# The first four activation tiles moved by 64 bytes within each partition

## The chip, the core and the metric

One core of one Trainium2 chip runs the whole program, once per launch. The metric is the device time of one execution in microseconds (us). Less is better.

## The reference, cut to what matters

The program is a two-layer transformer forward pass on 256 positions of width 2048, in float32. Nearly all of its arithmetic is in products of a 256-row activation with large weight matrices:

```python
def hybrid_mixer(h, w_in, ...):          # layer 1, first part
    p = h @ w_in                         # 2048 x 5136
    ...
    return jnp.concatenate([y_pool, y_dn], axis=-1) @ w_mix_out
def memory_cross_attention(h, mem_h, w_xq, w_xkv, w_xo):
    q = (h @ w_xq).reshape(...)
    kv = mem_h @ w_xkv                   # 2048 x 4096
    ...
    return o @ w_xo
def conv_glu_ffn(h, w_gate, w_up, conv_w, conv_b, w_down):
    gate = causal_dwconv(h @ w_gate, conv_w, conv_b)
    return (jax.nn.silu(gate) * (h @ w_up)) @ w_down
```

The second layer has the same form: an input projection (`w_in_2`), sparse and block attention, an output projection (`w_o_2`) and a feed-forward part of width 8192 (`w_up_2`, `w_down_2`). Around the products stand norms, short convolutions, a gated delta rule, softmaxes, and a modulation by six vectors from `w_ada_2`.

## The kernel before

**The split products.** Each float32 product is done as three passes in the fp32r type. An operand is split into a high part, rounded to fp32r, and a low part, the rest. High times high, high times low and low times high are added up in PSUM; low times low is left out. The split of a weight unit is done in `split_to`: ScalarE writes the high tile `wh` (L220), VectorE writes the low tile `wl` (L222). A unit is 128x1024 values, 512 KB of weights; SyncE's queue loads it into one of four `w32` buffers (L206), up to seven units ahead, and three buffers each of `wh` and `wl` hold split units.

**Two forms of product.** In `lin_b` (lines 320 to 322) a 128x128 block of the weight unit is the stationary operand and the activation, 128x256, is the moving one; the output is transposed. One unit gives 24 matmuls, in triples: `wh` with the high activation (L320), `wh` with the low activation (L321), `wl` with the high activation (L322). In `lin_a` (lines 302 to 304) it is the other way round: a 128x128 block of the activation is stationary and 512 columns of the weights move. Each matmul comes with its own load of the stationary operand into the array (LDWEIGHTS, shown as engine PEld), which runs while the matmul before it still streams.

```python
for b in range(4):
    ps = accs[b // 2][:, (b % 2) * T:(b % 2 + 1) * T]
    wb, wb2 = wh[:, k, b * P:(b + 1) * P], wl[:, k, b * P:(b + 1) * P]
    mm(ps, wb, h, start=kb == 0 and b % 2 == 0, stop=False, skip_group_check=True)
    mm(ps, wb, lo, start=False, stop=False, skip_group_check=True)
    mm(ps, wb2, h, start=False, stop=kb == g.nkb - 1, skip_group_check=True)
```

**The activation tiles.** `act_pair(0)` takes the tiles A0, A1 (high part, 16 blocks of 256 columns) and A2, A3 (low part), 8192 bytes per partition each; `act_pair(1)` takes A4 to A7 in the same way, which `hidden` also uses in pairs. A0 to A3 hold the input of every `lin_b` product but one: the four groups of memory keys (`mk`) read A4 to A7. A0 to A3 are also the stationary operand of some `lin_a` groups (`z0`, `z1`, `w_mix_out`, and the values `nv` and `mv` of layer 2). All other `lin_a` groups (memory values, `w_xo`, `w_down`, `w_o_2`, `w_down_2`) take A4 to A7.

**The order.** All engines' instructions are issued in program order from one Python loop; after each weight unit the loop steps the side tasks once (`pump`): evacuations, norms, attention, the modulation sums. So the tensor engine's queue is a series of units of 24 `lin_b` matmuls or 12 `lin_a` matmuls, with a few matmuls of the side tasks (tiles `m0` to `m3`) between two units.

**Where the tiles lie.** A pool gives each new tag the next free place in the partition, so the order of first use fixes the places, and `pad(name, n)` takes `n` float32 that nobody reads. Before, the byte offset modulo 256 is 128 for A0 to A3 (54656, 62848, 71040 and 79232), 192 for A4 to A7 (87488, 95680, 116416 and 124608), and 192 for all buffers of `wh`, `wl` and `w32` (188352 and up, 4096 bytes each). Between A3 and A4 lie two columns of 32 bytes, `c_mix_p` and `c_mem_p`. Within a tile, every 128-column weight block begins at a multiple of 512 bytes and every 256-column activation block at a multiple of 1024, so a block has its tile's offset modulo 256.

Of the kernel before, what the change touches and what calls it, by code (L numbers as in the profile page):

```python
# [90 lines left out]
class Prog:  # L91
# [409 lines left out]
    def run(self):  # L501
# [65 lines left out]
        self.mhalf = self.pool.tile([P, 8], F32, name="mhalf")  # L567
        nc.gpsimd.memset(self.mhalf, -0.5)
        nc.scalar.activation(self.col("first", 8), self.mhalf, AF.Copy)
        self.pad("pad0", 48)  # L570


        self.split_to(1)
# [9 lines left out]
        def stats():  # L583
            nc.sync.dma_start(cst, i["cst"])
            for c in range(4):
                nc.sync.dma_start(self.X[:, :, c * 512:(c + 1) * 512], xsrc[:, :, c * 512:(c + 1) * 512])
                yield
            self.load_small(w_in, 5120, 16, "ba", "s9")
            for n in ("dn_a_log", "dn_dt_bias"):
                t = self.named[n] = self.col(n, 8)  # L590
                sv = i[n]
                nc.sync.dma_start(t, bass.AP(tensor=sv.tensor, offset=sv.offset, ap=[[0, P], [1, 8]]))
            self.load_const("early")
            for c in range(4):
                for tb in range(2):
                    self.sq_sum(self.X[:, tb, c * 512:(c + 1) * 512], parts[:, tb, c:c + 1])
                yield
            yield from self.rms_task("mix_r", parts, "rr")
            msrc = i["mem"][0].rearrange("(b p) d -> p b d", p=P)
            for c in range(4):  # L600
                mt = self.t("r7", [P, 2, 512])
                nc.gpsimd.dma_start(mt, msrc[:, :, c * 512:(c + 1) * 512])
                for _ in range(3):
                    yield
                for tb in range(2):
                    self.sq_sum(mt[:, tb], mparts[:, tb, c:c + 1])
            self.rcm = self.rms_cols("mem_r", mparts)
            yield
            self.rrm = yield from self.row_bcast(self.rcm, "rrm", 1)

        st = self.start(stats())
        A4 = self.t("A4", [P, 2, 4, T])
        A5 = self.t("A5", [P, 2, 4, T])
        self.pad("pad1", 32)
        S = [{"k": A4[:, 0], "q": A4[:, 1], "v": A5[:, 0]}, {}]
        self.z = [None, None]
# [650 lines left out]
    def ffn1(self, xh, xl, ready, rt):  # L1267
# [6 lines left out]
        def ups(s):  # L1274
            hid[s] = self.hidden(["A4", "A6"] if s % 2 else ["A5", "A7"])
            j = 0
            for c in self.slabs[s]:
                self.lin_b(self.gate[c], xh, xl, lambda a, c=c: self.chain(self.wait_for(rt), self.gate_evac(a, c)),
                           ready=ready if c == 0 else None)
                self.lin_b(self.up[c], xh, xl, lambda a, c=c, j=j: self.up_evac(a, c, j, hid[s]))  # L1280
                j += 4
# [128 lines left out]
    def mixer2(self):  # L1410
# [42 lines left out]
        ev = self.lin_a(b2["nv"], xh, xl, lambda a: self.copy2_evac(a, vsw))  # L1453
        o0h, o0l = self.hidden(["A4", "A6"])
        att = []
# [378 lines left out]
    def ffn2(self):  # L1834
# [8 lines left out]
        def ups(s):  # L1843
            hid[s] = self.hidden(["A4", "A6"] if s % 2 else ["A5", "A7"])
            for c in range(2 * s, 2 * s + 2):
                self.lin_b(self.up2[c], xh, xl, lambda a, c=c: self.relu_evac(a, c, hid[s]),
                           ready=ready if c == 0 else None)
# [91 lines left out]
```

## Time and profile before

| | before |
|---|---|
| median of the runs | 2741.11 us (3 runs, 2740.76 to 2741.56) |
| the profiled execution | 2742.97 us |
| its span, first to last instruction | 2741.2 us |
| mean granted TensorE clock | 0.993 |
| tensor engine (PE) busy | 98% of the span |
| weight loads (PEld), VectorE (DVE), ScalarE (ACT), GpSimd (POOL) busy | 90%, 67%, 47%, 11% |
| read from HBM | 579.21 MB, 212 GB/s over the span |

The profile is of one execution. A matmul's duration is from its start to its modelled end and overlaps the next two matmuls; so durations add up to more than the span, and the pace of the engine is the spacing between starts. In a row of windows each window shows the busy time and, as (x...), the number of instructions that ran in it, those cut by its edges included.

### The profile page before, as it was taken

What the parts mean: (1) busy time and instruction counts of PE and PEld (TensorE: products, weight loads), DVE (VectorE), ACT (ScalarE), POOL (GpSimd) and SP (SyncE); (2) the same over time, 40 slices, a digit from 0 to 9 for tenths busy, and PEclk for the clock granted to TensorE, in tenths of its full rate; (3) what the DMA queues carried; (4) which work ended last, traced back from release to release, by engine and by line L of the source; (5) the groups of instructions that cost most, each with busy time, mean ns of one, the idle gap of its engine ahead of it and who ended that gap; (6) DMA issues with size and microseconds to landing.
All of it is one profiled execution on the core that took longest, in us unless ns stands there. A gap on an engine that the chain in (4) does not pass through costs nothing.

```text
span 2741.2 us, 45609 instructions
## 1 busy us (share of the span) xinstructions
PE 2683.0 (98%) x18322; PEld 2475.7 (90%) x18322; DVE 1848.6 (67%) x2276; ACT 1300.0 (47%) x1894; POOL 289.9 (11%) x249
## 2 busy tenths in 40 slices
PE   8999999999999999999999989999989999999997
PEld 8999998889989999999999789998879988999896
DVE  6665745677787877777877576677576566655556
ACT  6544533454455455444444454444554444444443
POOL 0230201000001020000000031101121000000020
PEclk9999999999999999999999999999999999999999
DMA  8644544688787877877877745443557767665554
GB/s 289 200 127 133 187 124 139 221 293 273 230 269 263 273 259 256 282 261 271 277 264 257 216 148 178 152 141 125 178 174 239 238 217 241 232 190 190 192 185 145
DMA packets 292116, 584.29 MB, mean 213 GB/s; under 512 B 23968, under 2 KB 32288, under 8 KB 291904
## 3 DMA queue, kind: packets, MB, share of 16 engines
q1 hardware_dynamic: 287952, 569.93, 63.5%
q0 software_dynamic: 3232, 10.14, 1.2%
q8 instruction: 143, 2.34, 0.3%
q10 hardware_dynamic: 720, 1.31, 0.1%
q14 instruction: 69, 0.57, 0.1%
HBM read 579.21 MB, written 2.10 MB: 212 GB/s over the span
## 4 chain that ended last, share of the span: by engine, by line
PE 89%; issue 6%; DVE 2%; ACT 1%; POOL 1%; DMA 0%; SPq 0%; DVEq 0%; ACTq 0%; POOLq 0%
PE acc L320 16%; PE acc L321 16%; PE acc L322 16%; PE acc L302 11%; PE acc L303 11%; PE acc L304 11%; PE m L992 1%; DVE wl L222 1%; PE m L1045 1%; PE m L1052 1%; ACT wh L220 1%; PE m L1142 1%; PE m L1111 1%; PE m L995 0%; DMA w<-w_in 0%
## 5 line engine op out<-in xcount | busy, mean ns | idle before, releaser
L222 DVE TENSOR_TENSOR wl<-w,wh 128x1024 fp32r<-128x1024 f32 x874 | 1094.3, 1254 | 826.4 <-ACT wh L220 820.0
L220 ACT ACTIVATE wh<-w 128x1024 fp32r<-128x1024 f32 x880 | 928.6, 1059 | 1152.7 <-PE acc L321 618.6
L320 PE MATMUL acc<-A,wh 128*128 128x256 f32 x3968 | 1125.1, 284 | 11.4 <-ACT A L406 7.7
L322 PE MATMUL acc<-A,wl 128*128 128x256 f32 x3968 | 1113.4, 281 | 6.1 <-POOL wl L222 3.3
L321 PE MATMUL acc<-A,wh 128*128 128x256 f32 x3968 | 1113.6, 281 | 0.4 <-DVE A L407 0.2
L320 PEld LDWEIGHTS acc<-A,wh 128*128 128x128 f32 x3968 | 752.0, 190 | 13.4 <-ACT A L406 7.7
L322 PEld LDWEIGHTS acc<-A,wl 128*128 128x128 f32 x3968 | 757.4, 191 | 6.7 <-POOL wl L222 3.7
L321 PEld LDWEIGHTS acc<-A,wh 128*128 128x128 f32 x3968 | 750.5, 189 | 2.2 <-DVE A L1406 0.6
L302 PE MATMUL acc<-wh,A 128*128 128x512 f32 x1536 | 608.6, 396 | 3.5 <-ACT wh L220 3.2
L303 PE MATMUL acc<-wl,A 128*128 128x512 f32 x1536 | 600.9, 391 | 2.2 <-DVE wl L222 2.2
L304 PE MATMUL acc<-wh,A 128*128 128x512 f32 x1536 | 600.6, 391 | 0.0
L303 PEld LDWEIGHTS acc<-wl,A 128*128 128x128 f32 x1536 | 289.4, 188 | 63.0 <-DVE wl L222 5.2
L302 PEld LDWEIGHTS acc<-wh,A 128*128 128x128 f32 x1536 | 289.1, 188 | 62.6 <-ACT wh L220 3.6
L304 PEld LDWEIGHTS acc<-wh,A 128*128 128x128 f32 x1536 | 289.1, 188 | 61.1
L1194 DVE SCALAR_TENSOR_TENSOR r<-r,c_silu_c,r 128x1024 f32<-128x1024 f32 x128 | 170.0, 1328 | 0.0
L1828 POOL TENSOR_TENSOR s<-s 128x512 f32<-128x512 f32 x32 | 51.0, 1593 | 557.2 <-ACT s L1827 557.2
L1194 DVE SCALAR_TENSOR_TENSOR s<-s,c_silu_c,s 128x512 f32<-128x512 f32 x128 | 95.8, 749 | 13.4 <-DMA s<-w_ada 11.6
L1249 POOL TENSOR_TENSOR r<-r,rr 128x1024 f32<-128x1024 f32 x11 | 27.9, 2534 | 571.8 <-ACT r L1248 529.0
L1672 ACT ACTIVATE s<-s,c_am 128x128 f32<-128x128 f32 (+1 forms) x48 | 21.5, 448 | 92.2 <-DVE c_am L1670 92.2
L1560 POOL TENSOR_TENSOR r<-r,s 128x512 f32<-128x512 f32 x15 | 25.5, 1703 | 227.4 <-DVE s L1557 227.4
L1245 DVE SCALAR_TENSOR_TENSOR r<-r,prm,r 128x254 f32<-128x254 f32 x88 | 42.3, 481 | 1.6
L378 ACT ACTIVATE dd<-X 128x512 bf16<-128x512 f32 x40 | 25.1, 627 | 23.2 <-DVE X L441 15.8
(368 smaller groups left out, 1634.7 us busy)
## 6 DMA issues: line engine op xcount, KB each, us to landing
w<-w_up SPq DMA_DIRECT2D x216, 512.0 KB, 3.7
w<-w_down SPq DMA_DIRECT2D x216, 512.0 KB, 4.0
w<-w_in SPq DMA_DIRECT2D x152, 512.0 KB, 3.5
r<-w_ada SPq DMA_DIRECT2D x128, 512.0 KB, 5.0
w<-w_gate SPq DMA_DIRECT2D x88, 512.0 KB, 4.3
w<-w_xkv SPq DMA_DIRECT2D x64, 512.0 KB, 3.9
s<-w_ada SPq DMA_DIRECT2D x128, 256.0 KB, 5.0
w<-w_mix_out SPq DMA_DIRECT2D x32, 512.0 KB, 3.6
```

The lines of the kernel that those rows point to most:

```text
L220: nc.scalar.activation(hi[:, :m], src[:, :m], AF.Copy)
L222: eng.tensor_tensor(lo[:, :m], src[:, :m], hi[:, :m].bitcast(F32), op=OP.subtract)
L302: mm(ps, h, wh[:, k, :], start=kb == 0, stop=False)
L303: mm(ps, h, wl[:, k, :], start=False, stop=False)
L304: mm(ps, lo, wh[:, k, :], start=False, stop=kb == g.nkb - 1)
L320: mm(ps, wb, h, start=kb == 0 and b % 2 == 0, stop=False, skip_group_check=True)
L321: mm(ps, wb, lo, start=False, stop=False, skip_group_check=True)
L322: mm(ps, wb2, h, start=False, stop=kb == g.nkb - 1, skip_group_check=True)
L1194: nc.vector.scalar_tensor_tensor(acc, tiles.pop(n), self.silu_c[:, kb:kb + 1], acc, op0=OP.mult, op1=OP.add)
L1245: nc.vector.scalar_tensor_tensor(cv[:, b, s:], st[:, b, :T - s], w[k], cv[:, b, s:], op0=OP.mult, op1=OP.add)
L1249: nc.gpsimd.tensor_tensor(cv, cv, self.rr[:, None, :].to_broadcast([P, 4, T]), op=OP.mult)
L1828: nc.gpsimd.tensor_tensor(y, y, y, op=OP.mult)
```

## The change

The pad ahead of A0 shrinks from 48 to 32 float32, and a new pad of 16 float32 stands between `c_mem_p` and A4:

```diff
-        self.pad("pad0", 48)
+        self.pad("pad0", 32)
...
         st = self.start(stats())
+        self.pad("pad3", 16)
         A4 = self.t("A4", [P, 2, 4, T])
```

A0 to A3 and the two 32-byte columns behind them begin 64 bytes earlier: A0 to A3 at 64 modulo 256. A4 and all tiles after it stay where they were. No instruction is added, removed or put in another order; the addresses in those that read or write A0 to A3, `c_mix_p` and `c_mem_p` are all that differs. Modulo 256, the distance from the weight buffers (192) to A0 to A3 goes from 64 to 128.

## Rows read from the trace of the kernel before

**Rows 1.** The profile's first part (busy time by engine) and its chain that ended last.
```profile
PE 2683.0 (98%) x18322; PEld 2475.7 (90%) x18322; DVE 1848.6 (67%) x2276; ACT 1300.0 (47%) x1894; POOL 289.9 (11%) x249
...
PE 89%; issue 6%; DVE 2%; ACT 1%; POOL 1%; DMA 0%; SPq 0%; DVEq 0%; ACTq 0%; POOLq 0%
```

**Rows 2.** Instruction groups of PE: shape, count, busy us, mean ns of one.
```profile
L320 PE MATMUL acc<-A,wh 128*128 128x256 f32 x3968 | 1125.1, 284 | 11.4 <-ACT A L406 7.7 <-ACT A L1401 3.5 <-ACT wh L220 0.2
L321 PE MATMUL acc<-A,wh 128*128 128x256 f32 x3968 | 1113.6, 281 | 0.4 <-DVE A L407 0.2
...
L302 PE MATMUL acc<-wh,A 128*128 128x512 f32 x1536 | 608.6, 396 | 3.5 <-ACT wh L220 3.2 <-DVE r L1258 0.3
```

**Rows 3.** Timeline of PE, three lin_b stretches; each pair is 8 spacings apart.
```profile
1299.74 0.28 PE L321 MATMUL acc<-A,wh 128*128 128x256 f32 x1
...
1300.65 0.28 PE L320 MATMUL acc<-A,wh 128*128 128x256 f32 x1
...
897.83 0.28 PE L321 MATMUL acc<-A,wh 128*128 128x256 f32 x1
...
898.77 0.28 PE L320 MATMUL acc<-A,wh 128*128 128x256 f32 x1
...
330.77 0.28 PE L321 MATMUL acc<-A,wh 128*128 128x256 f32 x1
...
331.73 0.28 PE L320 MATMUL acc<-A,wh 128*128 128x256 f32 x1
```

**Rows 4.** All engines in three windows of lin_b: us, then PE, PEld, DVE, ACT, POOL.
```profile
1300.00:1342.00 42.00, 42.00 (x373) 42.00 (x372) 33.61 (x37) 19.81 (x23) 0.79 (x1) 1.00 0.79 265
898.00:950.00 52.00, 52.00 (x443) 52.00 (x443) 42.70 (x46) 23.88 (x27) 2.44 (x1) 1.00 0.81 270
330.00:336.00 6.00, 6.00 (x52) 6.00 (x52) 2.56 (x3) 2.12 (x2) 0.00 (x0) 1.00 0.57 170
```

**Rows 5.** Line 321 alone, by stretch: PE busy (matmuls), PEld busy, clock, DMA.
```profile
13.00:236.00 223.00, 140.84 (x505) 94.96 (x505) 1.00 0.60 187
294.00:420.00 126.00, 72.45 (x256) 49.10 (x256) 1.00 0.48 146
613.00:1077.00 464.00, 251.22 (x894) 168.01 (x895) 1.00 0.79 263
1122.00:1212.00 90.00, 71.10 (x254) 47.72 (x255) 1.00 0.78 265
1256.00:1477.00 221.00, 141.74 (x511) 95.95 (x511) 1.00 0.81 273
1591.00:1863.00 272.00, 139.82 (x500) 94.90 (x500) 0.99 0.53 160
2016.00:2104.00 88.00, 69.22 (x251) 47.08 (x251) 1.00 0.72 238
2148.00:2637.00 489.00, 214.98 (x767) 144.01 (x767) 1.00 0.65 211
```

**Rows 6.** PEld groups in the windows 1300:1342, 898:950 (two rows) and 330:350.
```profile
L320 PEld LDWEIGHTS acc<-A,wh 128*128 128x128 f32 x124 | 23.3, 188 | 0.0
...
L320 PEld LDWEIGHTS acc<-A,wh 128*128 128x128 f32 x148 | 28.4, 192 | 0.0
L322 PEld LDWEIGHTS acc<-A,wl 128*128 128x128 f32 x148 | 27.8, 188 | 0.0
...
L322 PEld LDWEIGHTS acc<-A,wl 128*128 128x128 f32 x41 | 7.9, 192 | 0.0
```

**Rows 7.** Timeline of lin_a: first pair 9 spacings apart, second pair 10.
```profile
274.74 0.40 PE L303 MATMUL acc<-wl,A 128*128 128x512 f32 x1
...
276.81 0.39 PE L303 MATMUL acc<-wl,A 128*128 128x512 f32 x1
...
1229.67 0.39 PE L302 MATMUL acc<-wh,A 128*128 128x512 f32 x1
...
1231.94 0.39 PE L303 MATMUL acc<-wl,A 128*128 128x512 f32 x1
```

**Rows 8.** Writes of the activation tiles A, duration in ns min/median/max.
```profile
L406 ACT ACTIVATE A<-r,prm x32: 489/494/511, 7.1 to 300.9; 128x256 fp32r<-128x256 f32 x32
```

## Prediction

> **What bounds the kernel now.** I read the page first. The tensor engine is busy for 98% of the span, and the chain that ended last is PE for 89% [rows 1]. So the time is very nearly the number of matmuls times their spacing; a change of address can pay or cost only through the spacing, unless it slows a writer.
>
> Then the groups. The three lines of `lin_b` have 3968 matmuls each, of mean 281 to 284 ns, the three of `lin_a` 1536 each [rows 2]. A mean hides levels, so I looked at starts one after the other. Within one shape, with no wait between matmuls and the clock fully granted, there are three spacings [rows 3]: 0.91 us for eight starts (114 ns) around 1300 us, 0.94 us (117.5 ns) around 898 us, and 0.96 us (120 ns) around 331 us. The longer windows sharpen them. A window counts also what is in flight at its left edge, some 2.5 matmuls, so 42.00 us hold about 370.5 (113.4 ns), and 52.00 us about 440.5 (118.0 ns) [rows 4]. For the third I keep the 120 ns of the starts, since 6.00 us for 49.5 is too short to be better. With the levels go durations of 276, 281 and 283 ns, by which I can tell them in any row: 294 to 420 us has 72.45 us for 256, which is 283.
>
> The first two levels are A0 to A3 against the weights, 64 bytes apart modulo 256. The third, 120 ns, holds through all of 294 to 420 us: the only `lin_b` groups that read A4 to A7, at the same offset as the weights, distance 0. Loads of the stationary operand tell the same story: 188 ns each at 113.4 ns spacing; one line of the three at 192 ns at 118; at 120 ns the load of L322 has 192 ns as well [rows 6]. So I read the levels as two read streams of the tensor engine, the moving activation and the next weight block, getting into each other's way: always at distance 0; at distance 64 sometimes, in a manner that lasts for whole stretches.
>
> **How much time the 118 ns level takes.** Line 321 alone by stretch [rows 5]. Against 276 ns each, the seven stretches of A0 to A3 (all but 294 to 420) have: 140.84 - 505 x 0.276 = 1.5 us; 251.22 - 246.7 = 4.5; 71.10 - 70.1 = 1.0; 141.74 - 141.0 = 0.7; 139.82 - 138.0 = 1.8; 69.22 - 69.3 = -0.1; 214.98 - 211.7 = 3.3. Together 12.7 us on 3682 matmuls. One at the 118 ns level is 5 ns longer, so 12.7 / (3682 x 0.005) = 69% are at it. Three lines have 11046 matmuls; 69% of them by 4.6 ns of spacing (118.0 - 113.4) is 35 us. A few of those durations are long for other reasons (the stretch from 1591 has clock 0.99), so I take 33 us as what `lin_b` on A0 to A3 loses now against the 113.4 ns level.
>
> **The change part by part.**
>
> *The moving operand of lin_b.* The change removes and adds no instruction; it puts the moving operand of 11046 matmuls 128 bytes modulo 256 from the weights. No row shows this distance. Bounds from the nearest rows: all at 113.4 gives -33 us; all at 120, as at distance 0, gives 0.31 x 11046 x 6.6 ns = +22.6 and 0.69 x 11046 x 2.0 ns = +15.2, together +38 us. I take the lower end: from distance 0 to 64 the rows go from 120 ns throughout to 113.4 ns in part, 128 is the farthest that two offsets can be apart modulo 256, and a disturbance that fades with distance should be gone there.
>
> *What is behind it.* If PE goes faster, split units must come faster: 24 matmuls at 118.0 ns are 2.83 us, at 113.4 ns 2.72 us. In the window at 898 us DVE is busy 42.70 of 52.00 us (82%), ACT 46%, the DMA engines 81% [rows 4]. At 113.4 ns these become some 85%, 48% and 84%; the window at 1300 us already runs so, at 79% DMA and no idle PE. This cover stays. In stretches with many side matmuls (13 to 236 and 1591 to 1863 us) PE waits now and then for others, and part of the gain will be eaten there. Those hold 3.3 of the 12.7 us; with half of that lost, 13%, -33 becomes -29 us.
>
> *The stationary operand of lin_a.* The `lin_a` groups on A0 to A3 are 288 of the 1536 per line, 864 matmuls. At 275 us they are spaced 2.07 us / 9 = 230 ns, while groups on A4 to A7 at 1230 us have 2.27 / 10 = 227 ns [rows 7]. Here distance 0 is the better one, so the new distance may bring -3 ns or another +3 ns: -2.6 to +2.6 us. I take 0, for the two signs have equal support.
>
> *The writers.* ACT fills A0 to A1 and, later, A4 to A5 with the same instruction, 16 times each; over all 32 the duration is 489 to 511 ns [rows 8], so an offset of 128 or 192 makes no more than 22 ns. Most of these writes run beside matmuls; on the path stand a few at the start of each layer part, below 0.2 us. I take 0. The two 32-byte columns take sums of ACT and are read once each: 0.
>
> *The sum.* Span 2741.2 - 29 = 2712 us. The profiled execution took 2742.97, 1.8 more than its span, and the median is 1.9 below that; so the same 2712 for the median.
>
> The Trainium skill speaks against the whole change ("TensorE: Matmul & The Clock Gate", section "Step-by-step: what each phase is for"): the engine has two independent SBUF read ports, and loading the next weights does not take read bandwidth from the running matmul. By that page there would be nothing to gain from offsets, and the sum would be 0. The trace does not agree as far as spacing goes: one shape has 113.4, 118.0 and 120 ns in [rows 3, 4].
>
> **The rivals.**
>
> *No change: the offset is not the cause.* Which level a stretch has may be set by how the stretch begins (the first matmuls after side work) and the tiles' places may have nothing to do with it. For: at one and the same distance, 64, both levels occur, and they switch. Against: the 120 ns level belongs to A4 to A7 through 126 us and many interruptions, while no stretch of A0 to A3 has a mean above 281 [rows 5]. The time would be 2741, give or take 5 us for another draw of the levels. The rule of the Trainium skill named above ("TensorE: Matmul & The Clock Gate", same section) would give the same time; by the three spacings the trace speaks against it.
>
> *Slower: what counts repeats every 128 bytes.* Then 128 apart is as bad as 0 apart, all of `lin_b` runs at 120 ns, and the price is the +38 us above, less 2.6 us in `lin_a`: 2776 us. Place: L320 to L322 on A0 to A3. It decides as soon as the mean spacing there is over today's mean of 0.69 x 118.0 + 0.31 x 113.4 = 116.6 ns, a mean duration of 279.4 ns. For: distance 0 and 64 differ, and nothing in the rows shows that 64 and 128 aren't the two halves of one period. Against: two levels at distance 64 look like a middle case, not like the far end.
>
> *Slower by less: the 118 ns level becomes the lasting one.* If the new distance has both levels but falls into the 118 ns one nearly always, the 31% that have 113.4 ns now cost 4.6 ns each: 11046 x 0.31 x 4.6 = +16 us, 2757 us. For: stretches at 118 ns today tend to stay there (613 to 1077 us has a mean of 251.22 / 894 = 281 ns [rows 5]). Against: 2016 to 2104 us stays at 276 ns just as well.
>
> **How the numbers follow.** Forecast, 113.4 ns nearly everywhere: 0.48. No change: 0.17. 118 ns nearly everywhere: 0.18. The 128-byte repeat: 0.17. The predicted time is 2712, with 2706 to 2730 as its own range (all 33 us and the 2.6 of `lin_a` saved, or a third of the gain). A measurement of this kernel can tell some 0.2%, 5.5 us, from no change. Of the no-change case a little falls to either side, so faster is 0.49, same 0.15, slower 0.36. For 8 in 10 the range takes the forecast, the no-change case and the 118 ns case, and leaves the 120 ns case out: 2706 to 2762.
>
> **What would show it.** In the profile after: L320, L321 and L322 at a mean of 276 to 277 ns outside 294 to 420 us, all their loads at 188 ns, and windows like 898 to 950 us with 2.72 us for a unit of 24. From 294 to 420 us must stay at 283 ns, for neither A4 to A7 nor the weights move. DVE and ACT durations must not move. The forecast is wrong if the mean of L321 over A0 to A3 stays at 279 ns or rises; 283 ns with 192 ns loads would say that the repeat is 128 bytes, and 281 ns that the 118 ns level has won. The 113.4 ns level with an unchanged time would say that I misjudged the cover: then idle PE ahead of L320 with `wl` or `wh` as releaser must have grown.

## The result, and the profile after

| | before | after |
|---|---|---|
| median, timed in turn on one chip | 2741.16 us (4 runs, 2740.76 to 2741.56) | 2772.02 us (4 runs, 2771.12 to 2773.87) |
| span of the profiled execution | 2741.2 us | 2769.3 us |
| mean granted TensorE clock | 0.993 | 0.993 |

The ratio is 1.0111, with a 95% interval of 1.0099 to 1.0123: slower by 31 us. That is 60 us above the forecast, 10 us outside its range, and 4 us under the rival of a 128-byte repeat.

The page of after, the lines that answer to [rows 1] (busy time and count by engine; shares of the chain that ended last):

```profile
PE 2716.5 (98%) x18322; PEld 2507.4 (91%) x18322; DVE 1848.6 (67%) x2276; ACT 1300.6 (47%) x1894; POOL 288.8 (10%) x249
...
PE 89%; issue 6%; DVE 2%; ACT 1%; POOL 1%; DMA 0%; DVEq 0%; SPq 0%; ACTq 0%; POOLq 0%
```

PE is busy 33.5 us longer with the same 18322 matmuls. VectorE and ScalarE have the same busy time, and the clock is the same. PE's idle time went from 2741.2 - 2683.0 = 58.2 to 52.8 us, so 28 of the 33.5 us reach the span of these two executions. Nothing waits longer; the matmuls come more slowly. Which ones, the groups of after say (busy us, mean ns; as [rows 2]):

```profile
L320 PE MATMUL acc<-A,wh 128*128 128x256 f32 x3968 | 1131.6, 285 | 11.2 <-ACT A L406 7.7 <-ACT A L1402 3.5
L322 PE MATMUL acc<-A,wl 128*128 128x256 f32 x3968 | 1125.8, 284 | 5.8 <-POOL wl L222 3.1 <-DVE wl L222 2.7
L321 PE MATMUL acc<-A,wh 128*128 128x256 f32 x3968 | 1124.3, 283 | 0.1
L302 PE MATMUL acc<-wh,A 128*128 128x512 f32 x1536 | 609.2, 397 | 3.7 <-ACT wh L220 3.4 <-DVE r L1259 0.3
```

`lin_b` has it: L321 takes 10.7 us more than before, at a mean of 283 ns in place of 281 (the memory keys included in both). By stretch, L321 alone in four of the eight stretches (PE busy and matmuls, PEld busy and loads, clock, DMA share, GB/s; as [rows 5]):

```profile
296.00:422.00 126.00, 72.14 (x256) 48.85 (x255) 1.00 0.49 145
616.00:1085.00 469.00, 253.29 (x896) 168.82 (x896) 1.00 0.80 260
...
1265.00:1493.00 228.00, 143.93 (x511) 96.17 (x511) 1.00 0.81 265
...
2031.00:2126.00 95.00, 72.53 (x255) 48.79 (x256) 0.98 0.68 222
```

The first is the memory keys, which read A4 to A7: still 282 to 283 ns. The three others read A0 to A3 and have 253.29 / 896 = 283, 282 and 284 ns, where before they had 281, 277 and 276. The 284 is in part the clock: the granted clock was 0.5 (1.2 GHz) for 3.4 us at the start of that row, whose mean is 0.98; from 2036 us on, at 1.00, it is 69.43 us for 247, 281 ns. So the stretches that were at the best level lost most, some 5 ns against 2. The timeline of PE in after, each pair ten spacings apart, first on A0 to A3 (1.19 us, 119 ns), then in the memory keys (1.20 us, 120 ns):

```profile
909.83 0.28 PE L322 MATMUL acc<-A,wl 128*128 128x256 f32 x1
...
911.02 0.28 PE L320 MATMUL acc<-A,wh 128*128 128x256 f32 x1
...
330.76 0.28 PE L321 MATMUL acc<-A,wh 128*128 128x256 f32 x1
...
331.96 0.28 PE L322 MATMUL acc<-A,wl 128*128 128x256 f32 x1
```

Over all starts on A0 to A3 that follow each other within 140 ns (some 11,000), worked out from the trace, the mean spacing is 116.2 ns before and 119.2 after. 3.0 ns x 11046 = 33 us, about all that PE's busy time grew by. After is not the mix of 113.4 and 118, and not the steady 120 of the memory keys either: most single spacings lie between 115 and 122 ns.

Taken by group (the 192 matmuls that add up one set of outputs), after has two lasting levels as before has: 118.7 and 120.0 ns in place of 113.3 and 117.8. All engines in 20 us of two groups, first in before, then in the same two groups of after (columns as in [rows 4]):

```profile
1034.00:1054.00 20.00, 20.00 (x172) 20.00 (x172) 14.61 (x15) 8.58 (x9) 0.00 (x0) 1.00 0.80 277
2062.00:2082.00 20.00, 20.00 (x179) 20.00 (x179) 11.65 (x11) 9.61 (x12) 3.20 (x2) 1.00 0.77 247
...
1040.00:1060.00 20.00, 20.00 (x169) 20.00 (x168) 14.23 (x15) 8.58 (x9) 0.00 (x0) 1.00 0.82 268
2082.00:2102.00 20.00, 20.00 (x171) 20.00 (x170) 10.96 (x11) 9.31 (x11) 3.19 (x2) 1.00 0.75 239
```

Of the 58 groups on A0 to A3, all 13 that before has within 0.25 ns of 113.4 are at 118.7 in after, and of the 27 at 117.8, 21 are at 120.0. So the offset sets what the two levels are; which of the two a group gets goes largely with its place in the program.

Two more lines of after: the loads of one line in the window from 905 to 955 us, and the writers (as [rows 8]):

```profile
L320 PEld LDWEIGHTS acc<-A,wh 128*128 128x128 f32 x141 | 26.5, 188 | 0.0
...
L406 ACT ACTIVATE A<-r,prm x32: 489/494/512, 7.2 to 302.4; 128x256 fp32r<-128x256 f32 x32
```

At 119 ns the loads still take 188 ns, so a load's duration doesn't tell the level. The writers have not moved. In `lin_a` on A0 to A3, spacing went from 229.4 to 232.5 ns: 3.1 x 864 = 2.7 us. Starts of side matmuls that follow each other sum to 213.8 us in this execution of before and 209.4 in after, which takes more than that off again.

### The profile page after: what moved, and what is told of

It is laid out like the page before. It is cut to its first block, busy times and chain, and to the rows that moved or that the text cites. A ratio compares the mean times of both kernels' runs of the same rounds, so it can differ in the third digit from the quotient of the medians.

```text
span 2769.3 us, 45609 instructions
## 1 busy us (share of the span) xinstructions
PE 2716.5 (98%) x18322; PEld 2507.4 (91%) x18322; DVE 1848.6 (67%) x2276; ACT 1300.6 (47%) x1894; POOL 288.8 (10%) x249
## 4 chain that ended last, share of the span: by engine, by line
PE 89%; issue 6%; DVE 2%; ACT 1%; POOL 1%; DMA 0%; DVEq 0%; SPq 0%; ACTq 0%; POOLq 0%
PE acc L322 16%; PE acc L321 16%; PE acc L320 16%; PE acc L302 11%; PE acc L303 11%; PE acc L304 11%; PE m L993 1%; DVE wl L222 1%; PE m L1046 1%; PE m L1053 1%; PE m L1112 0%; PE m L1143 0%; ACT wh L220 0%; PE m L996 0%; PE m L1701 0%
## 5 line engine op out<-in xcount | busy, mean ns | idle before, releaser
L320 PE MATMUL acc<-A,wh 128*128 128x256 f32 x3968 | 1131.6, 285 | 11.2 <-ACT A L406 7.7
L322 PE MATMUL acc<-A,wl 128*128 128x256 f32 x3968 | 1125.8, 284 | 5.8 <-POOL wl L222 3.1
L321 PE MATMUL acc<-A,wh 128*128 128x256 f32 x3968 | 1124.3, 283 | 0.1
L320 PEld LDWEIGHTS acc<-A,wh 128*128 128x128 f32 x3968 | 754.0, 190 | 13.1 <-ACT A L406 7.7
L322 PEld LDWEIGHTS acc<-A,wl 128*128 128x128 f32 x3968 | 752.3, 190 | 6.4 <-POOL wl L222 3.5
L321 PEld LDWEIGHTS acc<-A,wh 128*128 128x128 f32 x3968 | 751.3, 189 | 1.9 <-DVE A L1407 0.6
```

## The experiments

"Distance" below is the weight tile's offset minus the activation tile's, modulo 256: 64 before, 128 after, 0 in the memory keys. "Spacing" is the mean on A0 to A3, worked out as above, from one start to the next. Edits are made to the kernel before, if nothing else is said. Each kernel was timed beside the kernel before, which had a median of 2738.0 to 2742.6 us; brackets after a ratio are its 95% interval.

### Is it the distance, and does it repeat after 128 bytes?

Two kernels put A0 to A3 at the other two multiples of 64; a third leaves A0 to A3 at after's place and moves everything behind them, the weights included, by the same 64 bytes.

```diff
# e1_at0 (e2_at192: no pad0, pad3 of 48)
-        self.pad("pad0", 48)
+        self.pad("pad0", 16)
...
         st = self.start(stats())
+        self.pad("pad3", 32)
# e3_all64
-        self.pad("pad0", 48)
+        self.pad("pad0", 32)
```

> A0 to A3 at 0 modulo 256, 64 bytes from the weights (192) on the other side than before; A4 and all later tiles unmoved. Theory D256 (the spacing follows the distance from moving to stationary operand modulo 256): a level of its own for this fourth distance; if it is the mirror of the kernel before, 2741 us, otherwise anything from 2710 to 2780. Theory D128 (the distance counts modulo 128): the same as before, 2741 within 6 us. Theory OWN (the offset of the moving tile itself counts, whatever the weights do): no tie to 2741.

> A0 to A3 at 192 modulo 256, at the same offset as the weights, distance 0 as in the memory-key groups. D256 and D128: lin_b on A0 to A3 goes to the 120 ns spacing of those groups (durations 283 ns, loads 192 ns), lin_a on them to 227 ns: about 2741 + 38 - 3 = 2776 us. D128 adds that this is the level of the changed kernel. OWN would allow another level.

> A0 to A3 at 64 as in the changed kernel, but without the second pad, so that A4 to A7, the weights and all tiles behind A3 move down by 64 bytes too: weights and A4 to A7 at 128, distance from A0 to A3 again 64 as before. Any theory of distance: as before, 2741 within 6 us. OWN: as the changed kernel, 2772 within 6 us.

Measured: at 0, 2755.6 us, 1.0055 [1.0035, 1.0076], spacing 117.7; at 192, 2776.8 us, 1.0130 [1.0111, 1.0150], spacing 119.9; all moved, 2739.2 us, 0.9996 [0.9985, 1.0006], spacing 116.2. The timeline of PE in the kernel with distance 0 (offset 192), 18 spacings in 2.16 us, and then the loads of L321 from 905 to 955 us:

```profile
904.79 0.28 PE L322 MATMUL acc<-A,wl 128*128 128x256 f32 x1
...
906.95 0.28 PE L322 MATMUL acc<-A,wl 128*128 128x256 f32 x1
...
L321 PEld LDWEIGHTS acc<-A,wh 128*128 128x128 f32 x140 | 26.9, 192 | 0.0
```

120.0 ns with 192 ns loads throughout: distance 0 gives A0 to A3 what it gives the memory keys, at the 2776 us that the prediction had worked out for 120 ns everywhere. With everything moved, after's place for A0 to A3 costs nothing. So the relative offset counts, not the tiles' own place. And the repeat is not 128 bytes: distance 192 (offset 0) ought then to be like 64, and it is 14 us slower, with nearly uniform spacings of 117 to 119 in place of the mix.

### What lies between?

Four kernels at the 32-byte steps, by the same two pads (`e6_at96` 40 and 8, `e7_at32` 24 and 24, `e8_at224` 8 and 40; `e9_at160` 40 and 8, with the two 32-byte columns moved ahead of `pad0`).

```diff
# e7_at32
-        self.pad("pad0", 48)
+        self.pad("pad0", 24)
...
+        self.pad("pad3", 24)
# e9_at160
-        self.pad("pad0", 48)
+        parts, mparts = self.parts("mix_p"), self.parts("mem_p")
+        self.pad("pad0", 40)
...
-        parts, mparts = self.parts("mix_p"), self.parts("mem_p")
...
+        self.pad("pad3", 8)
```

> A0 to A3 at 96 modulo 256, half way between the kernel before (128) and the changed one (64); everything else unmoved. Theory LINE (what counts is in which 64-byte piece a block begins): the same as at 64, 2772 us within 6. Theory FINE (the distance counts in steps below 64 bytes): between the two, 2745 to 2768 us, with a spacing of its own.

> A0 to A3 at 32 modulo 256, half way between 0 (2756 us, 117.7 ns) and 64 (2772 us, 119.2 ns). LINE: as at 0, 2756 us. FINE: between, 2756 to 2772 us.

> A0 to A3 at 160 modulo 256 (the two small columns go ahead of the pad), half way between 128 (2741 us, 116.2 ns) and 192 (2777 us, 119.9 ns). LINE: as at 128, 2741 us. FINE: between, 2741 to 2777 us; a spacing of 113.4 ns throughout would give 2712 us and a better place than any so far.

> A0 to A3 at 224 modulo 256, the last of the eight steps of 32 bytes, half way between 192 (2777 us) and 0 (2756 us). FINE, with what the other three half steps showed: a level of its own, 2755 to 2785 us. If the best distance were plus or minus 32 from the weights (160 is minus 32 and had 2762 us): under 2741 us.

All eight places together (weights at 192):

| A0 to A3 at | distance | us | ratio | spacing, ns |
|---|---|---|---|---|
| 128 (before) | 64 | 2741.2 | 1 | 116.2 |
| 224 | 224 | 2748.4 | 1.0027 [1.0017, 1.0037] | 116.8 |
| 0 | 192 | 2755.6 | 1.0055 [1.0035, 1.0076] | 117.7 |
| 160 | 32 | 2762.4 | 1.0077 [1.0060, 1.0094] | 118.3 |
| 96 | 96 | 2763.2 | 1.0079 [1.0064, 1.0094] | 118.3 |
| 64 (after) | 128 | 2772.0 | 1.0111 [1.0099, 1.0123] | 119.2 |
| 192 | 0 | 2776.8 | 1.0130 [1.0111, 1.0150] | 119.9 |
| 32 | 160 | 2780.3 | 1.0143 [1.0128, 1.0158] | 120.0 |

Steps of 32 bytes count, which the 64-byte theory denied; but the finer theory, by which a place lies between its neighbours, failed as well. Distance 160 is worse than both 128 and 192, distance 224 better than both 192 and 0. I found no formula over the distance, and which level belongs to which distance stays a table. The time does follow the spacing: 3.8 ns between the best and the worst row, by 11046, are 42 us, and the medians differ by 39.

### High and low tiles at different distances

The high tiles A0 and A1 (L320, L322) and the low ones A2 and A3 (L321) are set 64 bytes apart.

```diff
# e4_hi64: A0, A1 at 64; A2, A3 at 128 (e5_lo64: A2, A3 first, then pad3, then A0, A1)
-        a = [self.t(f"A{4 * half + j}", [P, 8, T], F32R) for j in range(4)]
+        a = [self.t(f"A{4 * half + j}", [P, 8, T], F32R) for j in range(2)]
+        if not half and "apart" not in self.named:
+            self.named["apart"] = self.pad("pad3", 16)
+        a += [self.t(f"A{4 * half + j}", [P, 8, T], F32R) for j in (2, 3)]
...
-        self.pad("pad0", 48)
+        self.pad("pad0", 32)
```

> Half of the change: A0 and A1 (high part, moving in two of three lin_b matmuls) at 64, A2 and A3 (low part, moving in one of three) stay at 128. If each matmul loses by its own moving tile, two thirds of the loss of 31 us: about 2762 us. If the load of the wl block, which runs beside the low part, were the one that collides, there would be no loss: 2741 us.

> The other half of the change: A2 and A3 (low part) at 64, A0 and A1 (high part) at 128, the weights at 192. With the high part alone at 64 the time was 2777 us, more than with both (2772). Theory EACH (each matmul loses by its own moving tile): one third of 31 us, 2751 us. Theory STEP (unequal offsets of high and low part are bad in themselves, since the moving stream then jumps in its place modulo 256 at every second matmul): 2770 to 2785 us.

Measured: 2776.9 us, 1.0129 [1.0105, 1.0153], and 2766.4 us, 1.0090 [1.0074, 1.0107]. Both miss all that was expected. Low at 128 and high at 64 is worse than all four at 64; its spacings, from a matmul's own start to the next, are 119.4, 121.2 and 119.2 ns for L320, L321 and L322, so the low tiles, which had not moved, have the longest. The three lines don't each bring the price of their own distance: both mixtures cost more than their share. This spoke for something that carries over from one matmul to the next.

### Is it the load beside the stream?

The other stream in the engine is the load of the next weight block. Three kernels shorten it: the stationary block has 32 columns in place of 128, and the matmul writes 32 output rows, so that three quarters of those products are left out. The moving operand and the number of matmuls stay. `e10_short` shortens two lines of three; the next two shorten all three lines of `lin_b` in all blocks but the first of a group.

```diff
# e10_short, on the kernel after
-                    mm(ps, wb, lo, start=False, stop=False, skip_group_check=True)
-                    mm(ps, wb2, h, start=False, stop=kb == g.nkb - 1, skip_group_check=True)
+                    mm(ps[:32], wb[:, :32], lo, start=False, stop=False, skip_group_check=True)
+                    mm(ps[:32], wb2[:, :32], h, start=False, stop=kb == g.nkb - 1, skip_group_check=True)
# e11_short_after and e12_short_before, ahead of the three mm
+                    n = 32 if kb else P
+                    ps, wb, wb2 = ps[:n], wb[:, :n], wb2[:, :n]
```

> The changed kernel, with the second and third matmul of each lin_b triple (L321, L322) using only the first 32 of 128 stationary columns, so that their loads are a quarter as long; the moving streams stay. It leaves out three quarters of these two passes. Theory LOAD (the moving stream loses while a load of the stationary operand runs): two of three collisions shrink to a quarter, the spacing of lin_b on A0 to A3 falls from 119.2 to 113.4 + 5.8 x (1 + 0.25 + 0.25) / 3 = 116.3 ns or less, the time to about 2740 us or less. Theory MOVING (the moving streams alone set the level): 119 ns and 2772 us as the changed kernel.

> The changed kernel, with all three matmuls of a lin_b triple using only 32 of 128 stationary columns in 15 of the 16 blocks of a product (three quarters of lin_b's outputs are left out there); moving streams and order stay. LOAD: the spacing on A0 to A3 is at most 113.4 + 5.8 / 4 = 114.9 ns, the time 2772 less 11046 x 4.3 ns = about 2724 us, and no more than 8 us above the same edit on the kernel before. MOVING: the difference of the two kernels of 31 us stays, at 2772 us here.

> The same shortening of all lin_b loads on the kernel before (A0 to A3 at 128). LOAD: spacing 113.4 + 2.8 / 4 = 114.1 ns, time about 2741 - 11046 x 2.1 ns = 2718 us, no more than 8 us under the changed kernel with this edit. MOVING: 2741 us, 31 us under it.

Measured: 2744.0 us, 1.0010 [1.0000, 1.0021], spacing 116.7; 2730.9 us, 0.9962 [0.9947, 0.9977], spacing 115.6; 2714.9 us, 0.9902 [0.9887, 0.9917], spacing 113.9. First two load groups of `e10_short`, from 905 to 955 us, then the timeline of `e12_short_before`, 19 spacings in 2.16 us:

```profile
L320 PEld LDWEIGHTS acc<-A,wh 128*128 128x128 f32 x143 | 26.9, 188 | 1.3
L322 PEld LDWEIGHTS acc<-A,wl 128*32 128x32 f32 x144 | 15.5, 108 | 1.1
```

```profile
904.74 0.28 PE L323 MATMUL acc<-A,wh 128*32 128x256 f32 x1
...
906.90 0.28 PE L324 MATMUL acc<-A,wl 128*32 128x256 f32 x1
```

Loads of 108 in place of 188 ns bring 113.7 ns by these two rows, the 113.4 ns level within their rounding; no group in any kernel here has a mean below 113.3. The load, or the writing of 128 output rows in place of 32, is thus a part of it, since the moving stream did not change; the next section tells the two apart. Between after and before there remained 16 us with short loads, where the theory of the load allowed 8 and that of the moving stream alone wanted 31. The 8 was worked out with loads a quarter as long, though, and they were 108 / 188 = 57% as long: a loss in proportion to the load's duration would have left 18 of the 31 us. So these three runs refute the theory of the moving stream alone, but not that of the load.

### Moving the loads instead of the stream

If the pair of stream and load counts, then the same must come from moving the load alone. First the short loads were displaced, by 192 bytes in after and by 64 in before (64 bytes either way, modulo 256), to other columns of the same weight block (so other products are computed; three quarters are left out as above):

```diff
# e13_after_c48, on the kernel after (e14_before_c16, on before: c = 16)
+                    n, c = (32, 48) if kb else (P, 0)
+                    ps, wb, wb2 = ps[:n], wb[:, c:c + n], wb2[:, c:c + n]
```

> The changed kernel with short loads as in e11_short_after, but of columns 48 to 79 of each block in place of 0 to 31, so that the load begins 192 bytes further on; A0 to A3, all tiles and the moving streams stay at the changed places. The distance from moving to loaded operand is then as in the kernel before (64 below). Theory PAIR (the level is set by the distance of the two streams that run side by side): the level of e12_short_before, 2715 us within 5, 113.9 ns. Theory PLACE (the offset of the moving stream itself, with the rest): as e11_short_after, 2731 us within 5, 115.4 ns.

> The kernel before with short loads of columns 16 to 47, which begin 64 bytes further on; all tiles where they were before, distance of moving to loaded operand 128 as in the changed kernel. PAIR: the level of e11_short_after, 2731 us within 5, 115.4 ns. PLACE: as e12_short_before, 2715 us within 5, 113.9 ns.

Measured: 2730.2 us, 0.9954 [0.9937, 0.9971], and 2712.7 us, 0.9895 [0.9880, 0.9910]. The times did not move, against the theory of the pair. The spacings did in after. All engines in 20 us of two groups that follow each other, first in `e11_short_after`, then in `e13_after_c48`:

```profile
980.00:1000.00 20.00, 20.00 (x176) 18.57 (x174) 15.97 (x12) 7.92 (x8) 3.23 (x2) 1.00 0.81 269
1002.00:1022.00 20.00, 20.00 (x176) 18.56 (x174) 18.70 (x21) 10.42 (x12) 2.43 (x1) 1.00 0.86 277
...
984.00:1004.00 20.00, 20.00 (x174) 18.42 (x172) 15.80 (x12) 7.91 (x8) 3.08 (x2) 1.00 0.81 270
1006.00:1026.00 20.00, 20.00 (x179) 19.03 (x178) 19.00 (x21) 10.46 (x12) 2.42 (x1) 1.00 0.85 277
```

With the short loads at their own places most groups run at 115.8 ns. Displaced, most go in turn at 116.8 and 113.7, whose mean is 115.3. That the two kernels take the same time is thus two different patterns with nearly one mean; no run shows a reason for it.

Then all loads at full length, each reading 128 columns that begin 16 columns (64 bytes) beside its block, so that neighbouring weight columns are multiplied; the work is all there, and no tile moves.

```diff
# e15_after_off192, on the kernel after: loads at 128 modulo 256
-                    wb, wb2 = wh[:, k, b * P:(b + 1) * P], wl[:, k, b * P:(b + 1) * P]
+                    o = k * g.n + b * P
+                    o += 48 if o == 0 else -16
+                    wb, wb2 = (w.rearrange("p k c -> p (k c)")[:, o:o + P] for w in (wh, wl))
# e16_before_off64, on the kernel before: loads at 0 modulo 256
+                    o += -48 if o == 896 else 16
```

> The changed kernel with full loads again (128 columns), each displaced in the weight tile by 192 bytes modulo 256 (16 columns earlier, for the first block of a unit 48 later), so each lin_b matmul uses neighbouring weight columns in place of its own. All tiles and moving streams stay at the changed places; the distance from moving to loaded operand is that of the kernel before. In the short-load runs one block in 16 still had full loads at the old places, which may have set the level for the 15 others. PAIR: 2741 us within 6, 113 to 118 ns mixed. PLACE: 2772 us within 6, 119 ns. In the memory keys the distance becomes that of e1_at0, which may take 2 us off in both.

> The kernel before with full loads displaced by 64 bytes modulo 256 (16 columns later, for the last block of a unit 48 earlier), so each lin_b matmul uses neighbouring weight columns. All tiles stay where they were before; the distance from moving to loaded operand is that of the changed kernel. PAIR: 2772 us within 6, 119 ns. PLACE: 2741 us within 6, 116 ns. In the memory keys up to 3 us less in both.

Measured: 2736.5 us, 0.9994 [0.9985, 1.0003], spacing 115.9; 2763.6 us, 1.0095 [1.0078, 1.0112], spacing 118.8. All engines from 905 to 955 us (PE, PEld, DVE, ACT, POOL, clock, DMA share, GB/s) in the kernel before, in the kernel after, in `e15_after_off192` and in `e16_before_off64`:

```profile
905.00:955.00 50.00, 50.00 (x427) 50.00 (x426) 41.06 (x44) 23.71 (x27) 2.44 (x1) 1.00 0.82 275
```

```profile
905.00:955.00 50.00, 50.00 (x424) 50.00 (x423) 41.29 (x44) 22.66 (x26) 2.39 (x1) 1.00 0.83 275
```

```profile
905.00:955.00 50.00, 50.00 (x443) 50.00 (x443) 42.87 (x46) 25.29 (x28) 2.81 (x2) 1.00 0.85 288
```

```profile
905.00:955.00 50.00, 50.00 (x424) 50.00 (x423) 40.59 (x44) 24.02 (x27) 2.40 (x1) 1.00 0.82 271
```

After with displaced loads starts 19 more matmuls in 50 us, PE never idle in either: (443 - 2.5) in 50 us are 113.5 ns, (424 - 2.5) are 118.6. This window is one in which `e15_after_off192` has the better level and before the worse (427); over all starts on A0 to A3, 119.2 ns became 115.9. By group the levels change places as well: after with displaced loads has 113.3 and 117.8 ns, the two of before, and before with displaced loads has 118.7 in most groups, the lower one of after. The load's address alone gives after's time back, and takes most of it from before: 22 of 31 us by the medians, 26 if each is set against the kernel before on its own chip (2763.6 - 2738.0), a little less than was expected. Some 3 us of the rest are hidden by the memory keys, which the same edit makes faster (119.8 to 115.8 ns, 768 matmuls). So the pair was right, for loads at full length.

The two kernels hold a test that I had not planned. Displaced loads also change the distance in the memory keys, whose activation tiles the change never touches: from 0 to 192 in the first, to 64 in the second. The timelines, 23 spacings each, 2.71 us (117.8 ns) in the first and 2.61 us (113.5 ns) in the second:

```profile
330.17 0.28 PE L324 MATMUL acc<-A,wl 128*128 128x256 f32 x1
...
332.88 0.28 PE L323 MATMUL acc<-A,wh 128*128 128x256 f32 x1
```

```profile
330.29 0.28 PE L324 MATMUL acc<-A,wl 128*128 128x256 f32 x1
...
332.90 0.28 PE L323 MATMUL acc<-A,wh 128*128 128x256 f32 x1
```

At distance 0 it was 120 ns. 117.8 is what distance 192 gave on A0 to A3 (117.7), and 113.5 is the better level of distance 64; over all memory keys the means are 117.8 and 115.8 ns, against 117.7 and 116.2 in the table. So two rows of the table hold for other tiles in another place. They also bear on the period: modulo 512, the distances of this 192 and of the one in `e1_at0` differ by 256 bytes, and the spacing is the same.

### Why did displaced short loads leave the time as it was?

In the kernels with short loads, the first block of each group still has full ones: 3968 - 3720 = 248 of 3968 per line, 6%. These were not displaced above. Now they alone are, by 64 bytes, and the short ones stay (three quarters of the short products are left out, and in the full ones neighbouring columns are multiplied).

```diff
# e17_after_set, on the kernel after (e18_before_set, on before: + (16 if kb == 0 else 0))
+                    n = 32 if kb else P
+                    o = k * g.n + b * P + ((-16 if b else 48) if kb == 0 else 0)
+                    ps, wb, wb2 = ps[:n], *(w.rearrange("p k c -> p (k c)")[:, o:o + n] for w in (wh, wl))
```

> The changed kernel with short loads as in e11_short_after (columns 0 to 31 at their own places, distance 128 to the moving operand), and only the full loads of the first of 16 blocks displaced by 192 bytes modulo 256 to the old distance. Theory SET (the full loads set the level, and the stream keeps it through the 15 blocks with short loads): the time of e12_short_before, 2715 us within 5. Theory RUN (each short load acts where it is): as e11_short_after, 2731 us within 5.

> The same on the kernel before: short loads at their own places (distance 64), the full loads of the first block displaced by 64 bytes to the distance of the changed kernel. SET: the time of e11_short_after, 2731 us within 5. RUN: as e12_short_before, 2715 us within 5.

Measured: 2714.7 us, 0.9899 [0.9885, 0.9914], spacing 114.0; 2728.3 us, 0.9945 [0.9929, 0.9962], spacing 115.3. The two kernels have changed places: after with displaced full loads stands where before with short loads stood (2714.9), and the reverse (2730.9). Instruction groups of the line `wh` with the low activation, first in `e17_after_set`, then in `e18_before_set`:

```profile
L324 PE MATMUL acc<-A,wh 128*32 128x256 f32 x3720 | 1031.1, 277 | 0.0
```

```profile
L324 PE MATMUL acc<-A,wh 128*32 128x256 f32 x3720 | 1033.6, 278 | 0.0
```

These are the short matmuls, which were not touched; they run slower when the 6% ahead of them stand at the other distance. All engines in 20 us of two groups that follow each other show it better, first `e17_after_set`, then `e18_before_set`:

```profile
982.00:1002.00 20.00, 20.00 (x179) 19.09 (x178) 14.83 (x12) 8.75 (x9) 1.98 (x2) 1.00 0.85 284
1004.00:1024.00 20.00, 20.00 (x179) 19.09 (x178) 19.07 (x22) 11.05 (x13) 2.41 (x1) 1.00 0.89 289
...
982.00:1002.00 20.00, 20.00 (x174) 18.42 (x172) 15.84 (x12) 7.91 (x8) 3.24 (x2) 1.00 0.82 272
1004.00:1024.00 20.00, 20.00 (x178) 19.03 (x178) 19.00 (x21) 10.46 (x12) 2.40 (x1) 1.00 0.85 274
```

The mean of each of the 15 blocks with short loads lies between 113.6 and 114.2 ns in the first kernel and between 114.9 and 115.3 in the second: it does not fade along the group. So the full loads at a group's beginning set a relation of stream and load that the rest of the group keeps. The address of the short loads is not without effect either: with the full loads at distance 128, groups run in turn at 116.8 and 113.7 ns when the short ones stand at 64 (here and in `e13_after_c48`), and at 115.8 when they stand at 128 (`e11_short_after`). With the full loads at 64, the spacing is 113.9 to 114.0 ns either way.

## Why the prediction was wrong

- **What bounds the kernel: right.** Spacing times count is the time. 3.0 ns x 11046 = 33 us is what PE's busy time grew by (33.5).
- **That the offset relative to the weights sets the level: right.** Moving everything kept the time (2739), moving loads alone moved it (2772 to 2736, 2741 to 2764). With VectorE and ScalarE both idle or both busy beside a matmul, spacing differs by less than 0.6 ns in before and by 0.2 in after, so these engines are not the cause. The rival of no change falls with that, for the time; its idea that a stretch's beginning decides which level it has is borne out by `e17_after_set` and `e18_before_set`. The Trainium skill ("TensorE: Matmul & The Clock Gate", section "Step-by-step: what each phase is for") says that loading the next weights takes no read bandwidth from the running matmul. The runs do not agree as far as time goes: the load's address alone is worth 36 and 22 us. Whether read bandwidth is what is lost, no run shows.
- **The bounds of lin_b, -33 to +38 us: right.** It came to +33.
- **The choice between them: the step that failed.** "I take the lower end: from distance 0 to 64 the rows go from 120 ns throughout to 113.4 ns in part, 128 is the farthest that two offsets can be apart modulo 256, and a disturbance that fades with distance should be gone there." It doesn't fade with distance. At 128 apart spacing is 119.2 ns, nearly the 119.9 of distance 0; 64 is the best of eight places, and 32 bytes on either side of it cost 21 and 22 us. Two points, 0 and 64, could not bear a line, and the kernel before happened to stand on the best one. The step cost the range too: its upper end left out the 120 ns case (2776 us), which had a chance of 0.17 and to which the time came within 4 us.
- **The rival of a 128-byte repeat: near in time by luck, wrong in cause.** It gave 2776 for 2772, but distances 64 and 192 differ by 14 us, 32 and 160 by 18.
- **The rival of a lasting 118 ns level: wrong.** After has neither of the two old levels of A0 to A3.
- **The signs to look for.** The mean of L321 tells the sign (281 to 283 ns over all its matmuls). "283 ns with 192 ns loads" came half: 283 with 188, so the load's duration was no sign to go by.
- **lin_a: the bound, not the 0 that I took.** It was said to be -2.6 to +2.6 us and became +2.7.
- **The cover and the writers: right as far as shown.** Nothing waited longer. In the kernels that ran at 113.4 ns over long stretches (`e12_short_before`, `e17_after_set`), the time is 2715 us, near the 2712 worked out for that level with some of it lost to waiting; but these kernels leave out products, and their memory keys are faster as well (114.5 to 115.0 ns). The size of the prize was right as far as that shows; no place of these tiles that was tried wins it.

**What stays open:** why the times stand in this order over the distance, and what inside the engine keeps the relation once it is set. That the two levels of before are two such relations fits the last two experiments and the levels by group, but nothing was tried that sets one of them on purpose at full loads. Why groups go in turn at two levels when full and short loads stand at different distances is open too. Steps below 32 bytes were not tried.

## What to carry to other kernels

Where matmuls follow each other without a gap and each brings its own load (188 ns here, at a spacing of 113 to 120), look at spacing from start to start: one shape can have several, and the offset of the moving operand relative to the stationary one is a size to be tuned (here 2741 to 2780 us, 1.4%, for no instruction changed). Scan it, all places of the ring, and keep the operands of one accumulation at one offset (both mixtures tried here cost more than their share); don't extrapolate from two points, for neighbours on either side can both be worse. To learn which of two streams is at fault, displace the other one by the same bytes and see if the time comes back. Then look at the levels by group as well: one time can hide two patterns.

## What the runs showed of the hardware that I had not expected

- Mean spacing of the fp32r matmul with 256 moving columns goes from 116.2 to 120.0 ns with the distance modulo 256 between the moving operand and the loads, a step of 32 bytes changes it, and the order is not monotone (the table). One distance can have two lasting levels: 113.3 and 117.8 ns at 64, 118.7 and 120.0 at 128.
- With the products of 512 columns and the activation as the load, the best distance is another one: 227 to 228 ns at distance 0, where `lin_b` is near its worst, 229.4 at 64, 232.5 at 128 and 233.2 at 192.
- The relation lasts: 6% of the loads set the pace of the other 94% (2731 to 2715 us and 2715 to 2728 us), while displacing those 94% left the time where it was (2730.9 to 2730.2 and 2714.9 to 2712.7), though in the first pair not the pattern of spacings.
- A load of 32 columns takes 108 ns in the profile and one of 128 columns 188; yet it is not the load's duration that sets the pace, for 188 ns goes with spacings of 113.5 as well as 118.6.
